# Strassen's seven products in three of eight row steps of an encoder layer's gate and up matrices, with PSUM, buffers and partial sums rearranged for it

## The chip, the cores and the metric

The kernel runs on one core of a Trainium2 chip. The metric is the time of one execution on the device in microseconds (us); the time of a kernel is the median of several runs. The profile was taken of one further execution. TensorE (PE) does the matmuls, VectorE (DVE) and ScalarE (ACT) the elementwise work, GpSimd (POOL) and SyncE (SP) issue DMAs, and POOL also does a few powers.

## The reference

The input is `x` of 256 rows and 2048 columns in float32. The layer is an FFN, a mixer with two attentions, and an FFN again, each with a norm before and after it. Cut to what matters here:

```python
def swiglu(h, w_gate, w_up, w_down):          # w_gate, w_up: 2048 x 5632, w_down: 5632 x 2048
    return (jax.nn.silu(h @ w_gate) * (h @ w_up)) @ w_down

f = swiglu(rmsnorm(x, ffn1_pre_g), ffn1_w_gate, ffn1_w_up, ffn1_w_down)
x = x + 0.5 * rmsnorm(f, ffn1_post_g)
h = rmsnorm(x, mix_pre_g)
proj = h @ w_in                               # 2048 x 8704: q, k, v of both attentions, gates ga, gb
...
merged = ga * (out_a @ w_proj_a) + gb * (out_b @ w_proj_b)
x = x + rmsnorm(merged @ w_out, mix_post_g)
f = swiglu(rmsnorm(x, ffn2_pre_g), ffn2_w_gate, ffn2_w_up, ffn2_w_down)
x = x + 0.5 * rmsnorm(f, ffn2_post_g)
```

## The kernel before

All weights come from memory once, as float32, and go through the same three steps. `load_upto` (L133) issues a DMA from SP of one unit, 256 rows by 512 columns (512 KB, as 128 partitions by 1024 elements), into one of four `raw` buffers. `emit_upto` (L142) splits the unit: ACT casts it to float32r, the high part (L152), and DVE subtracts that from the raw values, the low part (L154). Both go into the ten `w` buffers, five units. Activations are split in the same way, once, when they are transposed. A product is then three matmuls, high by high, low by high and high by low (`mm3`, L161 to L164), each of 128 x 128 activations that are loaded as weights of the array and 512 columns of the matrix that stream past.

`run_block` (L188) computes 512 columns for all 256 rows of the activations: two PSUM banks, one for each half `h` of 128 rows, and a loop over units of 256 matrix rows. A unit has two halves `j` of 128 rows, so it is 2 x 2 products, twelve matmuls. `weights(k)` emits two units ahead (`LA`). After the last unit `after(h, acc)` takes the bank: silu for a gate block (L349), the product with the silu for an up block (L353), a transposition through PSUM (`split_T`, L279 to L286), which is deferred by one unit, and so on.

`ffn` (L334) goes over the eleven column blocks of the gate and up matrices in two halves, six and five; a gate block has eight units, then the up block of the same columns. The transposed results are `hT`. After each half come four down blocks over the rows of that half. The results of the first half stay on the chip in `f` (ACT copy, L367), and those of the second are added to them on DVE (`finish_f`, L308), followed by the post norm. The mixer's 17 column blocks of `w_in`, two projections and `w_out` use `run_block` too. Its attentions are pipelines of small items that advance by one stage with each unit (`pump`).

PSUM has eight banks: four for blocks, two for transpositions, two for attention. The residual `x_sb` stays in its own buffers throughout. A scheduler orders each engine's instructions by program order as priority and by its own estimate of times; an engine then works in that order.

Of the kernel before, what the change touches and what calls it, by code (L numbers as in the profile page):

```python
# [11 lines left out]
F32 = mybir.dt.float32  # L12
# [23 lines left out]
SP0, SP1 = 3, 3  # L36
PACE0 = 5
AHEAD = 2
WARM = 7
# [3 lines left out]
def encoder_layer(  # L43
# [12 lines left out]
    xpool = ctx.enter_context(tc.tile_pool(name="xpool", bufs=1))  # L56
# [4 lines left out]
    t2p = ctx.enter_context(tc.tile_pool(name="t2p", bufs=6))  # L61
    bcp = ctx.enter_context(tc.tile_pool(name="bcp", bufs=2))
# [14 lines left out]
    def tp_tile():  # L77
        return tpp.tile([P, 4, P], F32, tag="tp", name=nm("tp"))

    def at_tile():  # L80
        return atp.tile([P, 2, 256], F32, tag="at", name=nm("at"))

    def t2():
        return t2p.tile([P, NC], F32, tag="t2", name=nm("t2"))

    def g4(shape, dt=F32R):
        return g4p.tile([P] + shape, dt, tag="g4", name=nm("g4"))
# [10 lines left out]
    x_sb = [xpool.tile([P, D], F32, name=f"x_sb{h}") for h in range(2)]  # L98
# [21 lines left out]
    def add_block(w, r0, nu, c0):  # L120
        start = len(units)
        for u in range(nu):
            units.append(w[r0 + 256 * u:r0 + 256 * u + 256, c0:c0 + NC])
        return start

# [6 lines left out]

    def load_upto(i):  # L133
        for k in range(len(loaded), min(i + 1, len(units))):
            loaded[k] = rawp.tile([P, 2, NC], F32, tag="raw", name=nm("raw"))
            c = units[k].shape[1]
            dst = loaded[k].rearrange("p a b -> p (a b)").rearrange("p (j c) -> p j c", c=c)
            src = units[k].rearrange("(j p) c -> p j c", p=P)
            for j in range(2) if k == 0 else (slice(None),):
                nc.sync.dma_start(dst[:, j], src[:, j])  # L140

    def emit_upto(i):  # L142
        for k in range(len(emitted), min(i + 1, len(units))):
            load_upto(k)
            raw = loaded[k]
            if k in spill:
                hi, lo = g4([2, NC]), g4([2, NC])
            else:
                hi = wp.tile([P, 2, NC], F32R, tag="w", name=nm("whi"))
                lo = wp.tile([P, 2, NC], F32R, tag="w", name=nm("wlo"))  # L150
            for j in range(2) if k == 0 else (slice(0, 2),):
                nc.scalar.copy(hi[:, j], raw[:, j])  # L152
                with queued(lo_of.get(0) if k in paced else None):
                    nc.vector.tensor_tensor(lo[:, j], raw[:, j], f32(hi[:, j]), ALU.subtract)  # L154
            emitted[k] = (hi, lo)
# [32 lines left out]
    def run_block(start, nu, lhs, after, lag=0, pre=None, tail=None):  # L188
        acc = [acc_tile(), acc_tile()]
        for i in range(nu + lag):  # L190
# [12 lines left out]
            for h, u in ((0, i), (1, i - lag)):  # L203
                if not 0 <= u < nu:
                    continue
                whi, wlo = weights(start + u)
                t = lhs(u, h)
                for j in range(2):
                    mm3(acc[h], t[:, 0, j, :], t[:, 1, j, :], whi[:, j, :], wlo[:, j, :],
                        u == 0 and j == 0, u == nu - 1 and j == 1)  # L210
                if u == nu - 1:
                    after(h, acc[h])
            pump()

    def quad(t, u):
        return t[:, :, 2 * (u % 2):2 * (u % 2) + 2, :]
# [14 lines left out]
    def make_xT(gi):  # L231
        done = set()

        def pre(u, h):
# [24 lines left out]
            if u % 2:  # L259
# [8 lines left out]
                else:  # L268
                    later(sq, 2)
# [9 lines left out]
    def split_T(src, n, name_shape):  # L279
# [3 lines left out]
        t = g4(name_shape)  # L283
        nc.scalar.copy(t[:, 0, :, :], tp[:, 0:n, :])  # L284
        nc.vector.tensor_tensor(t[:, 1, :, :], tp[:, 0:n, :], f32(t[:, 0, :, :]), ALU.subtract)  # L285
        return t  # L286

    def load_bc(src):
        t = bcp.tile([P, NC], F32, tag="bc", name=nm("bc"))
# [3 lines left out]
    def post_norm(f, r, h, final):  # L293
        def add_cols(c0, w):
            nc.vector.scalar_tensor_tensor(  # L295
                x_sb[h][:, c0:c0 + w], f[h][c0 // (2 * NC)][:, c0 % (2 * NC):c0 % (2 * NC) + w],
                r, x_sb[h][:, c0:c0 + w], ALU.mult, ALU.add)
# [4 lines left out]
        else:  # L302
            upd[h] = lambda u: add_cols(u * 256, 256)

    def finish_f(acc, f, gb, ss, h, n, add_prev, mul, add, final):
        fv = f[h][n // 2][:, (n % 2) * NC:(n % 2) * NC + NC]
# [27 lines left out]
    def ffn(post_g, pre, plan, lag, final, tail):  # L334
        hT = {}

        f = [[g4([2 * NC], F32) for _ in range(2)] for _ in range(2)]
        ss = [small(4, f"fss{h}") for h in range(2)]

        def lhs_h(off):  # L340
            return lambda u, h: quad(hT[(off + u) // 2, h], off + u)

        for half, (c_lo, c_hi) in enumerate(((0, 6), (6, 11))):
            for c in range(c_lo, c_hi):
                s = [None, None]

                def gate_after(h, acc, s=s):
                    s[h] = t2()
                    nc.scalar.activation(s[h], acc, AF.Silu, scale=r_pre[h])  # L349

# [405 lines left out]
```

## Time and profile before

| | |
|---|---|
| median of 3 runs | 2082.71 us (2082.37 to 2083.48) |
| the profiled execution | 2083.59 us |
| its span, first to last instruction | 2081.2 us |
| PE busy | 2064.4 us |
| DVE busy | 1141.7 us |
| ACT busy | 948.8 us |
| POOL busy | 24.5 us |
| moved by DMA | 393.40 MB |

Busy time is the time in which an engine executes instructions. A matmul's record lasts longer than the distance to the next one, because matmuls are pipelined; the rate is the distance between starts. An engine's idle time before an instruction is given with what ended it.

### The profile page before, as it was taken

Reading aid. Unit: us, or ns where it says so; the run is one execution under the profiler, and the core shown is the slowest. Engines: PE = TensorE matmul, PEld = TensorE weight load, DVE = VectorE, ACT = ScalarE, POOL = GpSimd, SP = SyncE. Lnnn points to the kernel's source line nnn. Section 1 sums busy time; section 2 is a strip of 40 time slices with the busy share of each in tenths; the row PEclk is TensorE's granted clock in tenths of the full one; section 3 lists DMA queues with packets and bytes.
Section 4 is the critical chain, followed back from the end, with each engine's and each line's share of the span. In section 5 each row is a group of like instructions: output and inputs, shape, how many; then the busy total and the mean of one; then the engine's idle time right before and its main releaser. Section 6 shows DMA issues by size and latency. Waiting matters only on the chain.

```text
span 2081.2 us, 24436 instructions
## 1 busy us (share of the span) xinstructions
PE 2064.4 (99%) x9373; PEld 1708.8 (82%) x9373; DVE 1141.7 (55%) x1330; ACT 948.8 (46%) x1205; POOL 24.5 (1%) x41
## 2 busy tenths in 40 slices
PE   9999999999999999999999999999999999999998
PEld 6888888888888878888888888888888888888886
DVE  5554444444445576767755555664445444455455
ACT  6444444444444455554644444554444444444442
POOL 1000000000000000000000000000000000000000
PEclk9999999999999999999999999999999999999999
DMA  8666655566665655555466666566665556666563
GB/s 258 200 189 186 192 192 192 192 193 190 189 189 196 198 168 187 171 163 172 152 196 198 197 204 198 182 193 191 192 191 188 189 196 193 189 189 191 187 204 125
DMA packets 203749, 393.40 MB, mean 189 GB/s; under 512 B 12447, under 2 KB 13265, under 8 KB 203633
## 3 DMA queue, kind: packets, MB, share of 16 engines
q1 hardware_dynamic: 203216, 391.17, 59.6%
q8 instruction: 73, 1.20, 0.2%
q0 software_dynamic: 384, 0.68, 0.2%
q14 instruction: 44, 0.35, 0.0%
q10 hardware_dynamic: 32, 0.01, 0.0%
HBM read 389.71 MB, written 2.10 MB: 188 GB/s over the span
## 4 chain that ended last, share of the span: by engine, by line
PE 63%; issue 34%; DMA 1%; DVE 1%; ACT 1%; POOL 0%; POOLq 0%; DVEq 0%; ACTq 0%
PE acc L163 20%; PE acc L164 20%; PE acc L162 20%; PE tp L282 1%; DMA raw<-in_w_in 0%; PE at L162 0%; PE at L163 0%; PE at L164 0%; DVE x_sb L295 0%; PE tp L246 0%; DMA sink<-in_sink_logit 0%; ACT whi L152 0%; DMA raw<-in_ffn_w_down 0%; DMA raw<-in_ffn_w_up 0%; DVE g L154 0%
## 5 line engine op out<-in xcount | busy, mean ns | idle before, releaser
L154 DVE TENSOR_TENSOR wlo<-raw,whi 128x1024 fp32r<-128x1024 f32 (+1 forms) x715 | 874.1, 1223 | 853.0 <-ACT whi L152 842.1
L152 ACT CAST whi<-raw 128x1024 fp32r<-128x1024 f32 (+1 forms) x715 | 752.0, 1052 | 974.6 <-PE acc L163 928.6
L163 PE MATMUL acc<-whi,xT 128*128 128x512 f32 x1928 | 754.1, 392 | 0.7 <-DVE xT L254 0.6
L162 PE MATMUL acc<-whi,xT 128*128 128x512 f32 x1928 | 754.1, 392 | 0.2 <-ACT whi L152 0.2
L164 PE MATMUL acc<-wlo,xT 128*128 128x512 f32 x1928 | 753.5, 392 | 0.0
L163 PEld LDWEIGHTS acc<-whi,xT 128*128 128x128 f32 x1928 | 362.7, 188 | 75.1 <-DVE xT L254 1.7
L162 PEld LDWEIGHTS acc<-whi,xT 128*128 128x128 f32 x1928 | 362.7, 188 | 74.1 <-ACT xT L252 0.8
L164 PEld LDWEIGHTS acc<-wlo,xT 128*128 128x128 f32 x1928 | 362.8, 188 | 73.1 <-DVE wlo L154 0.3
L162 PE MATMUL acc<-whi,g 128*128 128x512 f32 x928 | 361.3, 389 | 0.0
L163 PE MATMUL acc<-whi,g 128*128 128x512 f32 x928 | 361.3, 389 | 0.0
L164 PE MATMUL acc<-wlo,g 128*128 128x512 f32 x928 | 361.2, 390 | 0.0
L164 PEld LDWEIGHTS acc<-wlo,g 128*128 128x128 f32 x928 | 174.2, 188 | 36.2
L163 PEld LDWEIGHTS acc<-whi,g 128*128 128x128 f32 x928 | 174.2, 188 | 36.0
L162 PEld LDWEIGHTS acc<-whi,g 128*128 128x128 f32 x928 | 174.2, 188 | 35.9
L285 DVE TENSOR_TENSOR g<-tp,g 128x512 fp32r<-128x512 f32 (+1 forms) x68 | 42.2, 653 | 19.3 <-ACT g L284 19.3
L284 ACT CAST g<-tp 128x512 fp32r<-128x512 f32 (+1 forms) x68 | 35.4, 563 | 36.8 <-PE tp L282 36.4
L252 ACT ACTIVATE xT<-tp,gT 128x128 fp32r<-128x128 f32 x96 | 29.6, 367 | 25.7 <-PE tp L246 25.4
L349 ACT ACTIVATE t<-acc,pnr 128x512 f32<-128x512 f32 x44 | 30.2, 686 | 10.5 <-PE acc L164 10.5
L282 PE MATMUL tp<-ident,t 128*128 128x128 f32 x256 | 34.6, 272 | 0.0
L282 PEld LDWEIGHTS tp<-ident,t 128*128 128x128 f32 x256 | 30.2, 140 | 5.2
L254 DVE SCALAR_TENSOR_TENSOR xT<-tp,gT,xT 128x128 fp32r<-128x128 f32 x96 | 28.8, 344 | 8.3 <-ACT xT L252 7.5
L353 DVE SCALAR_TENSOR_TENSOR t<-acc,pnr,t 128x512 f32<-128x512 f32 x44 | 32.4, 748 | 0.0
(138 smaller groups left out, 598.7 us busy)
## 6 DMA issues: line engine op xcount, KB each, us to landing
raw<-in_ffn_w_up SPq DMA_DIRECT2D x176, 512.0 KB, 3.5
raw<-in_ffn_w_down SPq DMA_DIRECT2D x176, 512.0 KB, 3.8
raw<-in_ffn_w_gate SPq DMA_DIRECT2D x175, 512.0 KB, 3.5
raw<-in_w_in SPq DMA_DIRECT2D x136, 512.0 KB, 3.7
raw<-in_w_out SPq DMA_DIRECT2D x32, 512.0 KB, 4.5
raw<-in_w_proj_b SPq DMA_DIRECT2D x16, 512.0 KB, 4.3
raw<-in_w_proj_a SPq DMA_DIRECT2D x16, 512.0 KB, 4.4
bc<-in_ffn_post_g SPq DMA_DIRECT2D x8, 256.0 KB, 4.5
```

What stands on the lines that cost most here:

```text
L152: nc.scalar.copy(hi[:, j], raw[:, j])
L154: nc.vector.tensor_tensor(lo[:, j], raw[:, j], f32(hi[:, j]), ALU.subtract)
L162: nc.tensor.matmul(o, lhi, rhi, start=first, stop=False)
L163: nc.tensor.matmul(o, llo, rhi, start=False, stop=False)
L164: nc.tensor.matmul(o, lhi, rlo, start=False, stop=last)
L252: hi_of[h] = nc.scalar.activation(t[:, 0, j, :], tp[:, j, :], AF.Copy, scale=gs[j])
L254: lo_of[h] = nc.vector.scalar_tensor_tensor(t[:, 1, j, :], tp[:, j, :], gs[j], f32(t[:, 0, j, :]), ALU.mult, ALU.subtract)
L282: nc.tensor.transpose(tp[:, j, :], src[:, j * P:(j + 1) * P], ident)
L284: nc.scalar.copy(t[:, 0, :, :], tp[:, 0:n, :])
L285: nc.vector.tensor_tensor(t[:, 1, :, :], tp[:, 0:n, :], f32(t[:, 0, :, :]), ALU.subtract)
L349: nc.scalar.activation(s[h], acc, AF.Silu, scale=r_pre[h])
L353: nc.vector.scalar_tensor_tensor(hh, acc, r_pre[h], s[h], ALU.mult, ALU.mult)
```

## The change

The weight unit becomes 1 MB, 2048 elements a partition, in one of three kinds: `T` is 512 rows by 512 columns, `N` is 256 rows by 1024 columns, and `S` is also 256 rows by 1024 columns, but in four pieces of 128 x 512 for a Strassen step. There are four `raw` buffers and six `w` buffers, three units.

`run_wide` computes 1024 columns for all 256 rows: four results of 128 x 512. A plain step (`N`) is eight products, 24 matmuls. A Strassen step (`S`) takes the activations' and the weights' 2 x 2 pieces, and does seven products, 21 matmuls, into seven banks, with sums of the weight pieces (three additions on DVE, then the split) and sums of the activations' pieces (`make_forms`, once for each FFN and step). The products of all three Strassen steps of a block accumulate in the same banks, and the plain steps accumulate into four of them, since those are part of the four results. After the last `S` step, one copy on ACT and eight operations on DVE combine the banks in place, with priority, and the last two plain steps add onto the result.

Gate and up columns 512 to 5631 are done as five pairs of column blocks with the steps `NSNSNSNN`; column block 0 stays in `run_block`. Most other blocks become wide with plain steps alone. The down matrix is done in three parts of rows (column blocks 0 to 2, 3 to 6, 7 to 10) where there were two halves; the results of the first two parts go to memory, the second with an accumulating DMA, and are loaded before the third. `x` is loaded again from memory where it is needed, and after the post norm is written there. All PSUM tiles come from one pool of eight banks. The attention items and gates of the mixer are reordered; their computation stays. The diff, cut to its core:

```diff
+SKIND = "NSNSNSNN"
+HP = 300
+PARTS = ((0, 3), (3, 7), (7, 11))
-    wp = ctx.enter_context(tc.tile_pool(name="wp", bufs=10))
-    g4p = ctx.enter_context(tc.tile_pool(name="g4p", bufs=20))
+    wp = ctx.enter_context(tc.tile_pool(name="wp", bufs=6))
+    bigp = ctx.enter_context(tc.tile_pool(name="bigp", bufs=9))
-    accp = ctx.enter_context(tc.tile_pool(name="accp", bufs=4, space=bass.MemoryType.PSUM))
-    tpp = ctx.enter_context(tc.tile_pool(name="tpp", bufs=2, space=bass.MemoryType.PSUM))
-    atp = ctx.enter_context(tc.tile_pool(name="atp", bufs=2, space=bass.MemoryType.PSUM))
+    accp = ctx.enter_context(tc.tile_pool(name="accp", bufs=8, space=bass.MemoryType.PSUM))
...
     def emit_upto(i):
...
+            split(hi, lo, slice(0, 3))
+            nc.vector.tensor_tensor(raw[:, 1::2], raw[:, 1:3], raw[:, 3:4].to_broadcast([P, 2, NC]), ALU.add)
+            nc.vector.tensor_tensor(raw[:, 2], raw[:, 2], raw[:, 1], ALU.add)
+            nc.vector.tensor_tensor(raw[:, 0], raw[:, 0], raw[:, 2], ALU.add)
+            thi, tlo = pair("big")
+            split(thi, tlo, slice(0, 4))
+            emitted[k] = (hi, lo, thi, tlo)
...
+    def run_wide(block, lhs, forms, after):
...
+        for u, kind in enumerate(kinds):
+            w = weights(start + u)
+            if kind == "S":
+                t = lhs(u, 0), lhs(u, 1)
+                a11, a12, a22 = [(t[h][:, 0, j, :], t[h][:, 1, j, :]) for h, j in ((0, 0), (0, 1), (1, 1))]
+                fm = forms(u)
+                s1, s2, s3, s4 = [(fm[:, 0, i, :], fm[:, 1, i, :]) for i in range(4)]
+                ops = {"P1": (a11, w[0:2], 1), "P2": (a12, w[0:2], 0), "P3": (s4, w[0:2], 2),
+                       "Q5": (s1, w[2:4], 1), "P7": (s3, w[2:4], 3), "P6": (s2, w[2:4], 2), "Q4": (a22, w[2:4], 0)}
+                order = ("P1", "P2", "P6", "Q5", "P3", "P7", "Q4") if u == last_s else ("P1", "P2", "P3", "Q5", "P7", "P6", "Q4")
+                for o in order:
+                    f = open_(o)
+                    mm3s(bank[o], *ops[o], f, u == last_s, True)
+                if u == last_s:
+                    with tc.high_priority(HP):
+                        a, u2, v = t2(), t2(), t2()
+                        nc.scalar.copy(a, bank["P1"])
+                        nc.vector.tensor_tensor(bank["P2"], bank["P2"], a, ALU.add)
+                        nc.vector.tensor_tensor(u2, bank["P6"], a, ALU.add)
+                        nc.vector.tensor_tensor(v, bank["Q5"], u2, ALU.subtract)
+                        nc.vector.tensor_tensor(bank["P3"], bank["P3"], v, ALU.add)
+                        nc.vector.tensor_tensor(u2, bank["P7"], u2, ALU.add)
+                        if "X" in bank:
+                            nc.vector.tensor_tensor(v, bank["Q5"], u2, ALU.subtract)
+                            nc.vector.tensor_tensor(bank["X"], bank["X"], v, ALU.add)
...
+                        nc.vector.tensor_tensor(bank["Q4"], bank["Q4"], u2, ALU.add)
+            else:
+                order = (("P2", 0, 0), ("P3", 0, 1), ("X", 1, 1), ("Q4", 1, 0)) if last_s >= 0 else (("P2", 0, 0), ("P3", 0, 1), ("Q4", 1, 0), ("X", 1, 1))
+                for o, h, c in order:
+                    t = lhs(u, h)
+                    for j in range(2):
+                        f = open_(o)
+                        closes = u == end or u == last_s - 1 and o == "X"
+                        mm3s(bank[o], (t[:, 0, j, :], t[:, 1, j, :]), w, 2 * j + c, f, closes and j == 1, last_s >= 0)
+                    if u == end:
+                        with tc.high_priority(HP):
+                            after(h, c, bank[o])
             pump()
...
+    def reload_x(src):
+        for h in range(2):
+            x_sb[h] = big([D], F32)
+            nc.gpsimd.dma_start(x_sb[h], src[h])
...
+                later(tr, 2 if c0 + 1 in last_c or c0 == 0 else len(SKIND) - 1)
...
+            def down_after(h, c, acc, n, gb):
+                if not xlast:
+                    t = t2()
+                    nc.scalar.copy(t, acc)
+                    nc.gpsimd.dma_start(f_dram[h][:, (n + c) * NC:(n + c + 1) * NC], t,
+                                        accum_op=ALU.add if part else ALU.bypass)
+                else:
+                    finish_f(acc, f, gb[c], ss[h], h, n + c, True, 4.0 / D, 4.0 * EPS, final)
+            if xlast:
+                for h in range(2):
+                    f[h] = big([D], F32)
+                    nc.gpsimd.dma_start(f[h], f_dram[h])
```

`make_forms` does five additions or subtractions on DVE, one cast on ACT and one subtraction on DVE for each Strassen step, all of 512 elements a partition or less. The units that are split early at the border to the next stage (`spill`) were six of 512 KB and are one of 1 MB, and those held back (`paced`) were three and are one.

## Rows read from the trace of the kernel before

**Rows 1.** The page: busy time, share of the span and instructions of each engine.

```profile
PE 2064.4 (99%) x9373; PEld 1708.8 (82%) x9373; DVE 1141.7 (55%) x1330; ACT 948.8 (46%) x1205; POOL 24.5 (1%) x41
```

**Rows 2.** By stretch: us, busy PE, PEld, DVE, ACT, POOL, clock, DMA share, GB/s.

```profile
64.00:108.50 44.50, 44.50 (x202) 36.89 (x201) 22.37 (x21) 20.39 (x21) 0.00 (x0) 1.00 0.62 190
108.50:153.00 44.50, 44.50 (x202) 36.95 (x201) 22.38 (x21) 19.21 (x20) 0.00 (x0) 1.00 0.61 190
```

**Rows 3.** Order of time, PE: start us, duration us, line, tile; 36 matmuls apart.

```profile
100.09 0.39 PE L163 MATMUL acc<-whi,xT 128*128 128x512 f32 x1
...
108.25 0.39 PE L163 MATMUL acc<-whi,xT 128*128 128x512 f32 x1
```

**Rows 4.** The chain that ended last: two groups of transposes, start us, us.

```profile
64.19 0.87 PE tp L282 x8
108.64 0.87 PE tp L282 x8
```

**Rows 5.** Waits: who waited for whom, us in total, times, longest us.

```profile
ACT whi L152 <- PE acc L163: 928.6, 602, 2.6
DVE wlo L154 <- ACT whi L152: 842.1, 625, 2.5
...
PE acc L163 <- DVE xT L254: 2.2, 4, 0.8
```

**Rows 6.** By stretch, as rows 2: the start, the border to the mixer, the end.

```profile
0.00:20.00 20.00, 16.81 (x56) 10.61 (x57) 8.37 (x22) 11.02 (x26) 2.03 (x9) 1.00 0.90 304
720.00:760.00 40.00, 38.03 (x174) 30.24 (x173) 29.29 (x54) 20.31 (x37) 3.81 (x4) 1.00 0.54 172
...
2060.00:2081.00 21.00, 10.81 (x48) 8.63 (x46) 10.76 (x18) 0.00 (x0) 3.58 (x4) 0.87 0.29 100
```

**Rows 7.** Groups by shape: count, busy us, mean ns, idle before, releaser.

```profile
L154 DVE TENSOR_TENSOR wlo<-raw,whi 128x1024 fp32r<-128x1024 f32 x713 | 872.7, 1225 | 852.6 <-ACT whi L152 841.7 <-PE tp L282 5.9 <-PE at L164 0.9
...
L152 ACT CAST whi<-raw 128x1024 fp32r<-128x1024 f32 x713 | 750.7, 1054 | 972.4 <-PE acc L163 928.6 <-issue 21.8 <-ACT g L689 3.9
...
L353 DVE SCALAR_TENSOR_TENSOR t<-acc,pnr,t 128x512 f32<-128x512 f32 x44 | 32.4, 748 | 0.0
...
L308 DVE TENSOR_TENSOR g<-acc,g 128x512 f32<-128x512 f32 x16 | 11.0, 687 | 9.0 <-PE acc L164 8.7
...
L367 ACT COPY g<-acc 128x512 f32<-128x512 f32 x16 | 9.3, 583 | 4.3 <-PE acc L164 4.3
...
L481 DVE TENSOR_TENSOR t<-t,t 128x512 f32<-128x512 f32 x12 | 8.0, 683 | 0.0
...
L154 DVE TENSOR_TENSOR wlo<-raw,whi 128x512 fp32r<-128x512 f32 x2 | 1.4, 692 | 0.4 <-ACT whi L152 0.4
...
L152 ACT CAST whi<-raw 128x512 fp32r<-128x512 f32 x2 | 1.2, 619 | 2.2 <-DMA raw<-in_ffn_w_gate 2.2
```

**Rows 8.** Order of time, ACT and DVE: start us, duration, shape, idle time before.

```profile
101.19 1.05 ACT L152 CAST whi<-raw 128x1024 fp32r<-128x1024 f32 x1 [1.67 <-PE acc L163]
102.28 1.23 DVE L154 TENSOR_TENSOR wlo<-raw,whi 128x1024 fp32r<-128x1024 f32 x1 [1.50 <-ACT whi L152]
...
718.91 0.68 DVE L314 TENSOR_TENSOR g<-g,bc 128x512 f32<-128x512 f32 x1
719.52 0.15 DVE L316 TENSOR_REDUCE fss<-fss 128x1 f32<-128x3 f32 x1
...
724.97 1.23 DVE L154 TENSOR_TENSOR g<-raw,g 128x1024 fp32r<-128x1024 f32 x1 [1.69 <-ACT g L152]
726.12 1.22 DVE L154 TENSOR_TENSOR wlo<-raw,whi 128x1024 fp32r<-128x1024 f32 x1
```

**Rows 9.** DMA issues: out, in, queue, count, KB each, median us to landing.

```profile
raw<-in_ffn_w_up SPq DMA_DIRECT2D x176, 512.0 KB, 3.5
...
x_sb<-in_x SPq DMA_DIRECT2D x2, 512.0 KB, 9.2
...
rope<-in_c_rope POOLq DMA_DIRECT2D x1, 256.0 KB, 4.1
```

More of the change, by code (lines that the diff above doesn't have):

```diff
@@ L118, in encoder_layer, with add_units, add_tall, add_wide @@
     units = []
-    def add_block(w, r0, nu, c0):
+    def add_units(w, r0, rows, c0, kinds):
         start = len(units)
-        for u in range(nu):
-            units.append(w[r0 + 256 * u:r0 + 256 * u + 256, c0:c0 + NC])
-        return start
+        r = r0
+        for k in kinds:
+            n, c = (512, NC) if k == "T" else (256, 2 * NC)
+            units.append((k, w[r:r + n, c0:c0 + c]))
+            r += n
+        assert r == r0 + rows
+        return start
+    def add_tall(w, r0, rows, c0):
+        return add_units(w, r0, rows, c0, "T" * (rows // 512))
+    def add_wide(w, r0, rows, c0, kinds=None):
+        kinds = kinds or "N" * (rows // 256)
+        return add_units(w, r0, rows, c0, kinds), kinds
     loaded, emitted = {}, {}
@@ new lines, in run_block, with mm3s, open_ @@
+            if i % 2:
+                pump()
+    def mm3s(o, t, w, q, first, last, skip=False):
+        nc.tensor.matmul(o, t[0], w[0][:, q, :], start=first, stop=False, skip_group_check=skip)
+        nc.tensor.matmul(o, t[1], w[0][:, q, :], start=False, stop=False, skip_group_check=skip)
+        nc.tensor.matmul(o, t[0], w[1][:, q, :], start=False, stop=last, skip_group_check=skip)
+    def run_wide(block, lhs, forms, after):
+        start, kinds = block
+        last_s = kinds.rfind("S")
+        bank, opened = {}, set()
+        end = len(kinds) - 1
+        def open_(o):
+            if o not in bank:
+                bank[o] = acc_tile()
+            f = o not in opened
+            opened.add(o)
+            return f
+        for u, kind in enumerate(kinds):
[24 more added lines that the diff above has]
+                        else:
+                            nc.vector.tensor_tensor(bank["P1"], bank["Q5"], u2, ALU.subtract)
+                            bank["X"] = bank["P1"]
+                            opened.add("X")
+                        nc.vector.tensor_tensor(bank["Q4"], bank["Q4"], u2, ALU.add)
+            else:
+                order = (("P2", 0, 0), ("P3", 0, 1), ("X", 1, 1), ("Q4", 1, 0)) if last_s >= 0 else                     (("P2", 0, 0), ("P3", 0, 1), ("Q4", 1, 0), ("X", 1, 1))
+                for o, h, c in order:
+                    t = lhs(u, h)
+                    for j in range(2):
+                        f = open_(o)
[4 more added lines that the diff above has]
+                            after(h, c, bank[o])
@@ L453, in gains_T @@
             nc.vector.tensor_scalar_mul(gT[:, 48:50], gT[:, 48:50], 1.0 - LAM_INIT)
[L454 to L456 removed]
+        later(gains_T, 4)
+    later(constants, 4)
     pres = [make_xT(i) for i in range(3)]
     pres[0](0, 0)
[L459 removed]
+    ffn(ffn1_post_g, pres[0], plan1, 0, False, pres[1], [x_in[h * P:(h + 1) * P, :] for h in range(2)])
     roper = {}
```

441 lines of the change are left out of this document (247 added, 194 removed).

## The prediction

> **What bounds the kernel now.** I read the page's first two parts, then the table by stretch, then TensorE's own order of time, then the groups by shape, then the waits. The page gives TensorE (PE) 99% of the span, VectorE (DVE) 55% and ScalarE (ACT) 46% [rows 1]. That share is a mean, so I looked at the stretches where the change lies: there PE is busy for the whole of each, at a granted clock of 1.00, the higher of its two levels (2.4 GHz), with DVE busy half of the time [rows 2]. A busy PE could still be a slow one, so the cadence decides: the matmuls that start at 100.09 and 108.25 us are 36 apart, (108.25 - 100.09) / 36 = 0.2267 us each, without a gap [rows 3]. One gate block and one up block are 192 matmuls, 192 x 0.2267 = 43.5 us, and 0.87 for eight transposes makes 44.4; the distance of two such groups of transposes is 44.45 [rows 4]. So in these stages a matmul less is 0.2267 us less, as long as its operands come in time. The waits say that they do: ACT's casts wait for PE to give up weight buffers and DVE's subtractions for ACT, 929 and 842 us in all, while PE itself hardly appears as a waiting engine [rows 5]. PE is idle only at the start, by 2 us between the first FFN and the mixer, and at the end [rows 6].
>
> The profiled execution took 2083.59 us, 2.4 more than its span of 2081.2, and 0.9 more than the median of the runs shown. I make the sum against it.
>
> **What goes.** Gate and up columns 512 to 5631 are done in pairs of 512: five pairs, two matrices, two FFNs, 20 wide blocks. Three of their eight row steps use seven products where the plain step has eight; a product is three matmuls. That is 20 x 3 x 3 = 180 matmuls, 180 x 0.2267 = 40.8 us of PE [rows 3]. Nothing else on PE changes in number: the other wide blocks do the same matmuls in another order, and transposes and attention stay. 2083.6 - 40.8 = 2042.8.
>
> A page speaks for a smaller gain: the Trainium skill, "TensorE: Matmul & The Clock Gate", section "Wait — 56ns, not 53.3ns?", gives a warm start-to-start time of columns over 2.4 GHz plus about 2.5 ns, 215.7 ns at 512 columns, by which the 180 would be 38.8 us. The row has 226.7 ns at the same granted clock, so the trace disagrees and decides.
>
> **What DVE gets.** A row step now reads 256 x 1024 weights, 2048 elements a partition. The trace has no such shape; 512 and 1024 elements take 0.692 and 1.225 us [rows 7], so 512 more cost 0.533, and 1536 and 2048 come to 1.76 and 2.29. A plain step's low part: 2.29. A Strassen step: low parts of three of four pieces 1.76, three additions (1024, 512 and 512 elements, 1.225 + 0.683 + 0.683), low parts of the four sums 2.29: 6.65. A block has 5 x 2.29 + 3 x 6.65 = 31.4 us. At its last Strassen step eight operations combine the products, 8 x 0.687 = 5.5; their price stands on sums that read PSUM [rows 7], and writing PSUM is not in the trace, so 0.6 to 0.9 each. An up block adds four products with silu (0.748), and their four low parts after transposition (0.687, PSUM read too): 5.7. Gate and up together: 62.8 + 11.0 + 5.7 = 79.5 us of DVE. PE in that time: 2 x (5 x 24 + 3 x 21) = 366 matmuls, 83.0 us, and 1.7 of transposes: 84.7. So DVE stands at 94% by durations, where it is near 50% now.
>
> Durations overstate it. Where DVE is not kept waiting, a 512 operation that lasts 0.68 is followed 0.61 us later by the next, and a 1024 one after 1.15 [rows 8]. At these intervals the pair is some 75 us, 89%. The Trainium skill, "VectorE: DVE Perf Modes", section "The DRAIN you can't avoid", says that the next operation does not start until the pipe is empty; by that 79.5 would stand, and what could slip is 5 us a pair, not 10. The row sides with the shorter interval. Either way DVE's sum lies beside PE; ACT's does too: 1.92 a plain step, 1.49 + 1.92 a Strassen one (0.435 per 512 elements from 0.619 and 1.054 [rows 7]), 39.7 a pair, and with a dozen shorter casts and copies (0.583 to 0.619) under 50 of 84.7.
>
> **What can come late.** A sum that fits says nothing of the order. A Strassen step's chain is: ACT cast 1.49, DVE low 1.76, additions 2.4 at the intervals above, ACT cast of the sums 1.92, DVE low 2.29, and four handovers of 0.04, the time from the end of a cast to the next subtraction [rows 8]: 10.0 us. Weight buffers hold three row steps, so it starts when PE leaves the step three earlier: one plain and one Strassen step ahead, 45 x 0.2267 = 10.2 us. The sums are needed only after three products (2.0 us), or two in a block's last Strassen step (1.4), and their low part two matmuls later (0.45): slack 2.7 and 2.0 us. But DVE must fit the next plain step's 2.29 in too, and ACT its 1.92 cast; that cast starts 4.8 us in, ends at 6.7, the cast of the sums follows to 8.6, the plain low part ends at 9.0, the sums' low part at 11.3. The slack is then 0.7 us in the last Strassen step of a block and 1.4 in the others. After an up block the four silu products stand in front as well, and DVE ends its chain at about the time that the first Strassen step needs it. DVE is in order: behind each such chain stand the next low parts, and PE behind those.
>
> The combination is read by PE again: the plain step after it adds onto the combined banks. P1 and P2 are done 1.4 us into the last Strassen step and the first bank is needed at 4.8; the eight operations end about 7.9 if one plain low part got in ahead, where the fourth bank is asked for at 8.8, but the third only just in time, 7.3 against 7.5. So nothing to a microsecond a block.
>
> I take one DVE operation (0.4 us, between nothing and the 0.61 of a short one) late in each of 20 blocks, 8 us, and 2 us for the borders of blocks. The bounds: nothing, if the order fits everywhere; 60 x 0.61 = 37 us if every Strassen step comes one short operation late.
>
> **The rest, at nothing.** The forms of the activations: three steps, six DVE operations each, about 8 us an FFN, while DVE idles for half of an ordinary up block [rows 2]; without that cover 8 us. Partial sums go from ACT to memory by 32 DMAs of 256 KB from POOL's queue, where before 16 ACT copies (0.583) kept them on the chip [rows 7]. Accumulation in a DMA is in no row; plain 256 KB from the same queue took 4.1 us [rows 9]. They have a whole part, over 160 us, until the next accumulation, and the reload has a wide block, 43 us, where 512 KB of x took 9.2 at the crowded start [rows 9]. POOL's queue holds besides them only single-column powers. About 24 MB on 393 take the share of DMA time from 0.61 to 0.66 [rows 2]. A 1 MB load is between 3.5 us and twice that [rows 9]; the buffer of a Strassen step is free 1 to 2 us after PE enters it, and its successor is wanted over 8 us later. The tall first block loads 512 rows at once: the start is at 304 GB/s and bound by loads [rows 6], as many bytes come in almost the same order: 0, from -2 to +3. The border to the mixer has two large early units instead of twelve small: 0, from -1 to +4. Eight shared PSUM banks: a plain block holds four and hands over four, three of them early: 0 to 0.5 us in some 30 blocks.
>
> **Rivals.**
> (1) The gain is half eaten: DVE is late by 0.3 to 0.55 us in each of 60 steps, or the combination by 1.5 us in 20 blocks. 18 to 33 us: 2061 to 2077. For it: a slack of 0.7 us at 89 to 94% load. Against: the chain does not need DVE's whole lead in two of three steps.
> (2) Slower: DVE becomes the bound, by one mechanism. If in DVE's order a plain low part and its wait for the cast stand ahead of the sums (2.3 us), or the chain starts a short operation late each time, and the time is not won back because DVE's load leaves 0.9 us a Strassen step, each Strassen step holds PE. It saves 0.68 us, so from 0.68 us of delay a step the kernel is slower; at 1.2, 60 x 1.2 = 72: 2115. Against: DVE now idles 1.5 us before a subtraction, waiting for the cast and not for work [rows 8], and the room at the two plain steps that end a block makes good what was lost.
> (3) It gives nothing: the delays come to 0.6 to 0.75 us a step, 2079 to 2087.
>
> **How the numbers follow.** Forecast: 2083.6 - 40.8 + 10 = 2052.8, less 0.9 for the median: 2052, its own range 2041 to 2062, chance 0.56. Rival 1 has 0.25, rival 3 0.06, rival 2 0.12, and 0.01 lies below 2041. The range 2041 to 2076 takes in the forecast and nearly all of rival 1, about 0.8. A measurement of this kernel can tell 0.2%, 4.2 us, from no change: faster 0.82, same 0.06, slower 0.12.
>
> **What would show it.** PE's count down by 180 and its cadence in a gate block still 0.2267; about 85 us from pair to pair of gate and up where it is 88.9; DVE's busy time up from 1142 to about 1470 us, ACT's to about 1000; combining operations near 0.69 us. Delays of steps appear as PE waiting for DVE's sums at the first product that uses them, and as fewer casts waiting for PE; the combination appears as PE waiting for a DVE write of a bank. I am wrong if the interval of matmuls grows, if the operations into PSUM cost much over 0.9 us, if PE waits for DMA in the wide blocks, or if the gaps stand in stages that I set at nothing.

## The result and the profile after

| | before | after |
|---|---|---|
| median | 2082.61 us (2082.37 to 2083.48) | 2101.51 us (2097.97 to 2102.28) |
| after over before | | 1.0087, interval 1.0069 to 1.0104 |
| profiled execution | 2083.59 us | 2102.28 us |
| its span | 2081.2 us | 2100.5 us |

The forecast was 2052 with a range to 2076. The kernel became slower by 19 us, so forecast and range are both wrong.

The page after, as [rows 1] and [rows 9]: busy time of each engine, the DMA totals, and two groups of DMA issues (count, KB each, median us to landing).

```profile
PE 2045.2 (97%) x9193; PEld 1680.1 (80%) x9193; DVE 1430.9 (68%) x1400; ACT 987.4 (47%) x943; POOL 56.2 (3%) x91
...
DMA packets 140571, 416.36 MB, mean 198 GB/s; under 512 B 8415, under 2 KB 9233, under 8 KB 139185
...
raw<-in_ffn_w_down SPq DMA_DIRECT2D x88, 1024.0 KB, 5.2
...
f_dram<-t POOLq DMA_DIRECT2D x32, 256.0 KB, 5.8
```

PE has 9193 matmuls, 180 fewer. DVE rose to 1431 us and ACT to 987; 1470 and 1000 were forecast. 23 MB more were moved, where 24 were forecast. So the kernel does what the change says. The groups by shape of after, as [rows 7] (count, busy us, mean ns of one, idle time before and what ended it):

```profile
L179 DVE TENSOR_TENSOR w<-raw,w 128x2048 fp32r<-128x2048 f32 x301 | 689.1, 2289 | 416.5 <-ACT w L177 409.9 <-PE acc L258 5.1
L177 ACT CAST w<-raw 128x2048 fp32r<-128x2048 f32 x301 | 575.8, 1913 | 665.7 <-PE acc L258 513.8 <-PE acc L201 71.9 <-issue 37.8
...
L179 DVE TENSOR_TENSOR w<-raw,w 128x1536 fp32r<-128x1536 f32 x60 | 105.3, 1755 | 83.7 <-ACT w L177 55.9 <-issue 27.8
...
L188 DVE TENSOR_TENSOR raw<-raw 128x1024 f32<-128x1024 f32 x60 | 73.3, 1221 | 0.8
...
L190 DVE TENSOR_TENSOR raw<-raw 128x512 f32<-128x512 f32 x60 | 41.3, 688 | 0.9
...
L293 DVE TENSOR_TENSOR acc<-acc,t 128x512 f32<-128x512 f32 x20 | 13.9, 693 | 0.0
```

The prices that were worked out from smaller shapes hold: 2.29, 1.76, 1.22 and 0.69 us. An operation that writes PSUM in place takes 0.693, as one that only reads it did. The cadence holds too. In PE's order of time, these two matmuls of wide gate and up blocks are 332 apart, plain and Strassen steps between them (start us, duration):

```profile
249.86 0.39 PE L258 MATMUL acc<-w,xT 128*128 128x512 f32 x1
...
325.12 0.39 PE L259 MATMUL acc<-w,big 128*128 128x512 f32 x1
```

(325.12 - 249.86) / 332 = 0.2267 us, as [rows 3]. Not one price was wrong. What was wrong is the time that PE loses, idle or at the lower clock. The table by stretch of after, as [rows 2, 6] (us, busy PE, PEld, DVE, ACT, POOL, granted clock, DMA share, GB/s):

```profile
75.00:100.00 25.00, 21.37 (x86) 16.61 (x85) 20.29 (x15) 15.73 (x12) 0.00 (x0) 0.93 0.69 233
350.00:375.00 25.00, 25.00 (x112) 20.71 (x111) 24.69 (x18) 17.71 (x12) 0.00 (x0) 1.00 0.47 156
625.00:650.00 25.00, 23.06 (x95) 18.60 (x94) 21.18 (x19) 9.83 (x6) 2.17 (x4) 0.93 0.86 325
725.00:750.00 25.00, 21.23 (x87) 16.64 (x87) 17.48 (x26) 8.80 (x8) 4.03 (x4) 0.91 0.61 211
1000.00:1025.00 25.00, 18.52 (x84) 14.66 (x83) 16.72 (x21) 8.81 (x6) 0.00 (x0) 0.94 0.57 191
1425.00:1450.00 25.00, 21.33 (x80) 16.32 (x80) 19.46 (x17) 11.44 (x8) 0.00 (x0) 0.86 0.73 252
2079.00:2100.00 21.00, 8.64 (x39) 6.82 (x37) 10.00 (x18) 0.00 (x0) 3.57 (x4) 0.77 0.29 100
```

In 350 to 375 DVE is busy for 24.69 of 25 us, and PE is still never idle. The larger losses of this table are in single places: the first wide pair of each FFN (75, 1425), the first down weights after a wide block (625), the border to the mixer (725), one place in the mixer (1000), and the end.

To put a number on each stage I summed, over PE's whole order of time, the distance from start to start less 0.2267 us for each matmul of 512 columns, half of that for one of 256, and 0.109 for each transposition (0.87 / 8 [rows 4]). This is PE's lost time, whether it idles or runs at the lower clock. The stages are the start (to 50 us), the two FFNs, the border to the mixer, the mixer, and the border to the second FFN; a border lasts from 5 us before the first transposition of the rows for the next norm to 1 us after the last. The end is from the last matmul's start. All in us, profiled executions; the kernels e1 to e11 come below.

| | before | after | e1 | e2 | e3 | e4 | e5 | e6 | e11 |
|---|---|---|---|---|---|---|---|---|---|
| start | 9.3 | 9.9 | 9.5 | 9.8 | 10.3 | 10.8 | 9.9 | 9.8 | 9.4 |
| FFNs | 0.7 | 35.9 | 0.5 | 23.5 | 20.2 | 34.4 | 16.3 | 0.5 | 51.1 |
| border to mixer | 3.7 | 10.2 | 10.7 | 7.6 | 11.7 | 9.6 | 7.3 | 7.9 | 7.3 |
| mixer | 2.5 | 13.3 | 13.3 | 12.6 | 13.3 | 9.2 | 2.7 | 2.7 | 2.7 |
| border to FFN 2 | 2.0 | 6.5 | 6.8 | 6.7 | 6.5 | 6.6 | 6.3 | 6.7 | 6.4 |
| sum | 18.1 | 75.8 | 40.7 | 60.1 | 62.1 | 70.5 | 42.6 | 27.6 | 76.9 |
| end | 10.8 | 13.3 | 13.2 | 12.9 | 13.5 | 13.2 | 12.8 | 12.8 | 12.2 |

From before to after: 57.6 more lost (75.77 - 18.14), 2.5 more at the end, 40.8 saved: +19.3, the difference of the spans.

### The profile page after: what moved, and what is told of

It is laid out like the page before. It is cut to its first block, busy times and chain, and to the rows that moved or that the text cites. A ratio compares the mean times of both kernels' runs of the same rounds, so it can differ in the third digit from the quotient of the medians.

```text
span 2100.5 us, 22846 instructions
## 1 busy us (share of the span) xinstructions
PE 2045.2 (97%) x9193; PEld 1680.1 (80%) x9193; DVE 1430.9 (68%) x1400; ACT 987.4 (47%) x943; POOL 56.2 (3%) x91
## 5 line engine op out<-in xcount | busy, mean ns | idle before, releaser
L179 DVE TENSOR_TENSOR w<-raw,w 128x2048 fp32r<-128x2048 f32 (+2 forms) x365 | 796.5, 2184 | 500.3 <-ACT w L177 465.8
L177 ACT CAST w<-raw 128x2048 fp32r<-128x2048 f32 (+2 forms) x365 | 666.7, 1828 | 783.8 <-PE acc L258 605.4
L257 PE MATMUL acc<-w,xT 128*128 128x512 f32 x1368 | 536.6, 393 | 5.6 <-ACT t L292 4.0
L258 PE MATMUL acc<-w,xT 128*128 128x512 f32 x1368 | 534.1, 390 | 0.0
L259 PE MATMUL acc<-w,xT 128*128 128x512 f32 x1368 | 512.5, 391 | 0.6 <-DVE w L179 0.6
L257 PE MATMUL acc<-w,big 128*128 128x512 f32 x828 | 323.2, 391 | 3.3 <-ACT w L177 3.3
L258 PE MATMUL acc<-w,big 128*128 128x512 f32 x828 | 323.8, 391 | 0.0
L259 PE MATMUL acc<-w,big 128*128 128x512 f32 x828 | 317.6, 390 | 0.2 <-DVE w L179 0.2
L257 PEld LDWEIGHTS acc<-w,xT 128*128 128x128 f32 x1368 | 257.5, 188 | 61.9 <-ACT t L292 4.8
L259 PEld LDWEIGHTS acc<-w,xT 128*128 128x128 f32 x1368 | 257.5, 188 | 54.8 <-DVE w L179 1.4
L258 PEld LDWEIGHTS acc<-w,xT 128*128 128x128 f32 x1368 | 257.6, 188 | 52.0
L257 PEld LDWEIGHTS acc<-w,big 128*128 128x128 f32 x828 | 155.7, 188 | 36.4 <-ACT w L177 4.1
L259 PEld LDWEIGHTS acc<-w,big 128*128 128x128 f32 x828 | 155.6, 188 | 32.5 <-DVE w L179 0.6
L258 PEld LDWEIGHTS acc<-w,big 128*128 128x128 f32 x828 | 155.7, 188 | 31.9
L177 ACT CAST big<-raw 128x2048 fp32r<-128x2048 f32 x62 | 118.6, 1913 | 93.1 <-DVE raw L190 89.1
L179 DVE TENSOR_TENSOR big<-raw,big 128x2048 fp32r<-128x2048 f32 x62 | 141.2, 2286 | 20.7 <-ACT big L177 15.8
L201 PE MATMUL acc<-w,xT 128*128 128x512 f32 x208 | 83.0, 401 | 3.0 <-DVE xT L358 3.0
L200 PE MATMUL acc<-w,xT 128*128 128x512 f32 x208 | 82.0, 399 | 0.0
L202 PE MATMUL acc<-w,xT 128*128 128x512 f32 x208 | 80.4, 393 | 0.0
L257 PE MATMUL acc<-big,big 128*128 128x512 f32 x180 | 72.3, 402 | 6.1 <-ACT big L177 6.1
L200 PE MATMUL acc<-w,big 128*128 128x512 f32 x192 | 74.7, 389 | 0.0
L201 PE MATMUL acc<-w,big 128*128 128x512 f32 x192 | 74.7, 389 | 0.0
```

What stands on the lines that cost most here:

```text
L177: nc.scalar.copy(hi[:, sl], raw[:, sl])
L179: nc.vector.tensor_tensor(lo[:, sl], raw[:, sl], f32(hi[:, sl]), ALU.subtract)
L200: nc.tensor.matmul(o, lhi, rhi, start=first, stop=False)
L201: nc.tensor.matmul(o, llo, rhi, start=False, stop=False)
L202: nc.tensor.matmul(o, lhi, rlo, start=False, stop=last)
L257: nc.tensor.matmul(o, t[0], w[0][:, q, :], start=first, stop=False, skip_group_check=skip)
```

## The experiments

Each is an edit of the changed kernel and does the whole computation. Each is measured against the kernel before on the same chip in the same session (medians of before: 2082.50 for e1 to e4, 2082.41 for e5 to e8, 2082.09 for e9 to e11).

### e1: the rearrangement alone

```diff
-SKIND = "NSNSNSNN"
+SKIND = "NNNNNNNN"
```

> All eight row steps of every gate and up pair are plain (the step string is NNNNNNNN), all else as in the changed kernel. Theory A: PE's time in the gate and up pairs falls by 40.8 us of matmuls and rises by some 27 us of stalls there, and the rearrangement outside the Strassen steps costs some 32 us; so without Strassen 2101.5 + 40.8 - 27 = 2115 (2111 to 2119). Rival B: the whole loss comes from the load that Strassen puts on DVE, and the rearrangement is free: 2083 (2079 to 2088).

Measured: 2109.07 us (2107.98 to 2109.16), 1.0124 of before, 1.0109 to 1.0139. So everything but Strassen's products costs 26.6 us, and Strassen's 180 matmuls less bring 2109.07 - 2101.51 = 7.6 us instead of 40.8. The table by stretch of e1:

```profile
75.00:100.00 25.00, 25.00 (x112) 20.70 (x111) 9.84 (x5) 9.02 (x5) 0.00 (x0) 1.00 0.56 182
625.00:650.00 25.00, 25.00 (x112) 20.70 (x111) 10.91 (x5) 7.96 (x5) 0.00 (x0) 1.00 0.52 181
1000.00:1025.00 25.00, 20.43 (x93) 16.34 (x91) 15.92 (x19) 8.81 (x6) 0.00 (x0) 0.98 0.57 191
```

The FFNs are full again (0.5 in the table of stages, 0.7 before), also at 625, where the partial sums are loaded back. The mixer's hole stays, and so do the borders and the end. Two causes, then: 35 us of lost PE time (75.8 - 40.7) that comes with Strassen's steps, and 25 that comes with the rest (40.7 - 18.1, and 2.4 at the end). Rival B, a free rearrangement, is out; theory A had it right in kind, with 2111 at the least.

### e3: the forms of the activations earlier

```diff
-                    gate_up(0, ..., lambda a: run_block(plan["up"][0], KU, lhs_x, a))
-                    make_forms(SKIND)
+                    def first_up(a):
+                        make_forms(SKIND)
+                        run_block(plan["up"][0], KU, lhs_x, a)
+                    gate_up(0, ..., first_up)
```

> The sums of the activations' pieces (make_forms) are written ahead of the first up block instead of behind it, all else as in the changed kernel. Theory A: the stalls in the first wide pair of each FFN, some 6 us each with the lower clock that follows, come from these 8 us of DVE work falling together with the first Strassen steps: 2089 to 2093. Rival B: the first pair is slow by its own chain or its loads, not by the forms: 2099 to 2102.

Measured: 2088.50 us (2087.17 to 2090.94), 1.0027 of before, 1.0018 to 1.0037: 13.0 us less than after. DVE's order of time shows when the last low part of the forms ends, first in after, then in e3:

```profile
79.03 0.68 DVE L402 TENSOR_TENSOR big<-t,big 128x512 fp32r<-128x512 f32 x1
```

```profile
55.04 0.69 DVE L402 TENSOR_TENSOR big<-t,big 128x512 fp32r<-128x512 f32 x1
```

The prediction hid these 8 us in the half-idle DVE of the first up block. But the change writes them behind that block, and program order is the scheduler's priority: in after, the first of them starts at 60.80 and they run between the sums of the first wide block. That block then gets its own operations late. DVE, then ACT, then PE of after (in brackets, the idle time before and what ended it):

```profile
88.87 2.29 DVE L179 TENSOR_TENSOR w<-raw,w 128x2048 fp32r<-128x2048 f32 x1
91.08 0.69 DVE L190 TENSOR_TENSOR raw<-raw 128x512 f32<-128x512 f32 x1
91.68 2.29 DVE L179 TENSOR_TENSOR w<-raw,w 128x2048 fp32r<-128x2048 f32 x1
```

```profile
89.44 1.90 ACT L177 CAST w<-raw 128x2048 fp32r<-128x2048 f32 x1 [0.75 <-DMA raw<-in_ffn_w_up]
91.24 0.58 ACT L292 COPY t<-acc 128x512 f32<-128x512 f32 x1
91.80 1.90 ACT L177 CAST big<-raw 128x2048 fp32r<-128x2048 f32 x1
```

```profile
91.87 0.50 PE L257 MATMUL acc<-w,xT 128*128 128x512 f32 x1 [2.19 <-ACT t L292]
...
93.75 0.79 PE L257 MATMUL acc<-big,big 128*128 128x512 f32 x1 [1.14 <-ACT big L177]
```

A whole low part (2.29) stands ahead of the last sum, L190, and the sums' cast follows that. A whole cast (1.90) stands ahead of the copy that PE waits for. In e3 PE loses 0.7 us in 75 to 100 and nothing in 1425 to 1450; in after it lost 5.9 and 6.8 there.

### e4: no empty pipeline ahead of the attention items

```diff
     run_wide(pm["qa"], lhs_x, None, q_after(qaT))
-    drain()
     ticker[0] = pipeline([ItemA(h, p) for h in range(2) for p in range(4)], (0, 1, 2))
```

> The drain after the qa block is left out, so that the transposes of its four results come one step of the next block later; all else as in the changed kernel. Theory A: the 9.4 us that PE loses there wait for four rotations on DVE that nothing covers; with a step of 5.4 us ahead of them, 5 to 8 us come back: 2093 to 2097. Rival B: the rotations only move and PE waits as long behind the step: 2100 to 2102.

Measured: 2095.98 us (2094.69 to 2096.93), 1.0060 of before, 1.0044 to 1.0077: 5.5 us less than after. `drain` does all deferred work before the items start: the transpositions of four rotated results, with no matmuls of a block between them. PE and DVE of after at that place:

```profile
1018.01 0.66 PE L407 MATMUL tp<-ident,t 128*128 128x128 f32 x4 [1.10 <-DVE t L648]
1021.46 0.82 PE L407 MATMUL tp<-ident,t 128*128 128x128 f32 x4 [2.80 <-DVE t L648]
1024.86 1.97 PE L407 MATMUL tp<-ident,t 128*128 128x128 f32 x8 [2.58 <-DVE t L648]
```

```profile
1020.72 0.68 DVE L648 TENSOR_TENSOR t<-t,t 128x512 f32<-128x512 f32 x1
1021.32 2.29 DVE L179 TENSOR_TENSOR w<-raw,w 128x2048 fp32r<-128x2048 f32 x1
```

Three waits on DVE, 6.5 us, and in the last of them a whole low part stands ahead of the next rotations. The line is not new: in the kernel before, the same `drain` stands behind the second of two blocks of 512 columns, and its transpositions (974.28 and 975.49) wait for nothing. The change put one wide block with four rotations ahead of it. Without `drain` PE is busy for all of 1000 to 1025. The mixer's stage gives 4.1 of the 5.5 us; 1.5 stand in the FFNs, which the edit doesn't touch. Some of the gain is given back in the attention items, where a small operation now has a whole low part ahead of it (e4, DVE, then PE):

```profile
1075.39 2.28 DVE L179 TENSOR_TENSOR w<-raw,w 128x2048 fp32r<-128x2048 f32 x1
...
1077.66 0.42 DVE L807 TENSOR_TENSOR big<-at,big 128x256 fp32r<-128x256 f32 x1
```

```profile
1078.23 0.51 PE L200 MATMUL at<-t,big 128*128 128x256 f32 x1 [2.70 <-DVE big L807]
```

### e2, e7, e9: smaller pieces of the split

e2 casts and subtracts 1024 elements at a time, as before the change, while loads and steps stay as they are. e7 halves the subtractions alone, e9 the casts alone. The core of e2:

```diff
-                for j in ... if k == 0 else [slice(0, 4)]:
+                for j in ... if k == 0 else [slice(0, 2), slice(2, 4)]:
                     split(hi, lo, j)
...
-            split(hi, lo, slice(0, 3))
+            split(hi, lo, slice(0, 2))
+            split(hi, lo, slice(2, 3))
...
-            split(thi, tlo, slice(0, 4))
+            split(thi, tlo, slice(0, 2))
+            split(thi, tlo, slice(2, 4))
```

and of e7 (e9 does the same to the cast in place of the subtraction):

```diff
                 nc.scalar.copy(hi[:, sl], raw[:, sl])
-                with queued(lo_of.get(0) if k in paced else None):
-                    nc.vector.tensor_tensor(lo[:, sl], raw[:, sl], f32(hi[:, sl]), ALU.subtract)
+                for a in range(sl.start, sl.stop, 2):
+                    q = slice(a, min(a + 2, sl.stop))
+                    with queued(lo_of.get(0) if k in paced else None):
+                        nc.vector.tensor_tensor(lo[:, q], raw[:, q], f32(hi[:, q]), ALU.subtract)
```

> Casts and subtractions of the weights in pieces of 1024 elements, as in the kernel before, instead of 2048; loads, steps and all else as in the changed kernel. Theory A: a part of the stalls comes from pieces of 2.29 us that stand in DVE's order ahead of a short operation that PE waits for; halving them gives back a third to a half of the 56 us of stalls added: 2075 to 2090. Rival B: DVE's load decides; more operations make it higher: 2101 to 2106.

> DVE's subtractions of the weights in pieces of 1024 elements, ACT's casts left at 2048; all else as in the changed kernel. Theory A: it is DVE's long piece ahead of short operations that costs: most of e2_halves' 15 us comes back, 2087 to 2092. Rival B: it is the length of the chain, in which a subtraction waits for a whole cast: casts of 2048 leave it as it was, 2096 to 2102.

> ACT's casts of the weights in pieces of 1024 elements, DVE's subtractions left at 2048, the counterpart of e7_dve_halves; all else as in the changed kernel. Theory A: what helps is that a subtraction of the first half runs beside the cast of the second, which shortens the chain and needs both halved: 2099 to 2103. Rival B: it is ACT's long cast that stands ahead of short casts and copies: most of e2_halves' 15 us comes back, 2086 to 2092.

Measured: e2 2086.37 us (2084.84 to 2087.88), 1.0017 of before, 1.0008 to 1.0027, 15.1 less than after, though DVE's busy time rose by 27 us to 1458. e7 2102.37 (2101.68 to 2104.17), 1.0096, 1.0080 to 1.0111; e9 2100.35 (2099.03 to 2102.82), 1.0085, 1.0070 to 1.0100: no gain from either alone. After e2 I held that DVE's long pieces ahead of short operations are the whole cause. By that e7 should have had most of e2's gain, so that theory fell.

The stages tell more than the medians. The FFNs lose 28.9 us in e7 and 27.7 in e9, against 35.9 in after and 23.5 in e2. Each half alone does help there, by 7 to 8 us, and the mixer takes most of it back: 20.2 in e7 and 19.5 in e9, against 13.3. DVE, then PE of e7 at the largest of these places:

```profile
965.80 2.72 DVE L838 SCALAR_TENSOR_TENSOR t<-acc,pnr,t 128x512 f32<-128x512 f32 x4
968.43 2.35 DVE L181 TENSOR_TENSOR w<-raw,w 128x1024 fp32r<-128x1024 f32 x2
...
971.57 0.48 DVE L738 TENSOR_SCALAR t<-at,br 128x256 f32<-128x256 f32 x1 [0.47 <-POOL br L329]
```

```profile
972.11 0.69 PE L748 MATMUL tp<-ident,t 128*128 128x128 f32 x2 [4.67 <-DVE t L738]
```

Two halves in a row are no shorter than a whole when nothing is put between them (2.35 us here, 2.29 for a whole). The edit changed the scheduler's order, and at this place to a worse one: four gate operations and both halves ahead of the 0.48 us for which PE waits (4.67; in after 1.48). What can be said is that pieces of 1024 on both engines bring 15 us, of which the FFNs have 12 and the borders and the mixer 3. With both halved, the subtraction of the first half can run beside the cast of the second. How much of e2's gain is that shorter chain and how much is a luckier order, these three runs don't separate.

### e5 and e6: the three together, and with plain steps

e5 has the edits of e2, e3 and e4; e6 has them and the SKIND of e1.

> The three edits together: pieces of 1024 elements, forms ahead of the first up block, no drain after the qa block. Theory A: they cure different stalls, so the gains add: 2101.5 - 15.1 - 13.0 - 5.5 = 2068 (2064 to 2073), below the kernel before. Rival B: the first two cure the same stalls (late chains in the first wide pairs), so that about half of the smaller is lost: 2074 to 2081.

> As e5_three, with plain steps alone. Theory A: in good order the Strassen steps lose little of their 40.8 us of matmuls, some 10 us; plain steps are then about 30 us slower than e5_three: 2095 to 2100. Rival B: DVE's load in the Strassen blocks eats the gain whatever the order, as it did at 2109 against 2101.5: 6 to 14 us slower than e5_three.

Measured: e5 2069.59 us (2068.65 to 2070.30), 0.9937 of before, 0.9924 to 0.9949; e6 2093.93 (2093.18 to 2094.79), 1.0054, 1.0040 to 1.0068. The three gains add up in the total, 15.1 + 13.0 + 5.5 = 33.6 against 31.9 measured, and the change becomes a gain: 12.8 us, where the forecast had 31. That the total came out is luck in part, since theory A's reason doesn't hold by stage. In the FFNs the three gain 12.4, 15.7 and 1.5 us apart, 29.6, and 19.6 together: there they cure the same stalls, as rival B had it. In the mixer they gain 4.8 apart and 10.6 together. Strassen's steps now bring 2093.93 - 2069.59 = 24.3 us of 40.8; the FFNs still lose 16.3. The first row of PE's waits in e5 (us in total, times, longest):

```profile
PE acc L261 <- DVE big L179: 5.1, 9, 0.6
```

Nine short waits for the sums' low part, of 0.5 to 0.6 us: this is the late operation that the prediction priced. e6 still stands 11.5 us above before. By the table of stages that is the borders (4.2 and 4.7) and the end (2.0), and the mixer has no part in it any more (0.2).

### e8 and e10: the end and the borders

e8 splits the last unit early; e10 is e8 and lets the second half of the rows lag by three steps where it was two.

```diff
         spill.add(b)
         paced.add(b + 3)
+    spill.add(len(units) - 1)
```

```diff
-LAG = 2
+LAG = 3
```

> As e5_three, and the last weight unit of the kernel is split into buffers of its own, as the last ones of the kernel before were. Theory A: the first half of the rows is finished earlier ahead of the second, and the tail of 13.2 us from the last matmul to the end comes back to the 10.8 of before: 2 to 3 us less than e5_three. Rival B: the tail is set by DVE's order there and not by the unit: as e5_three, within 1 us.

> As e8_three_spill, with a lag of three row steps instead of two between the halves of the rows at the two borders into the next norm. Theory A: PE waits at the borders because too few matmuls of the second half lie behind the first half's norm (10 to 14 where before there were 18); six more matmuls give 1 to 1.4 us at each border: 2066 to 2068. Rival B: the weights of three units leave no buffer for the next, so that the gain is lost again or more: 2069 to 2074.

Measured: e8 2069.12 us (2067.66 to 2069.58), 0.9933 of before, 0.9920 to 0.9945; it can't be told from e5. Its end takes 12.0 us where that of e5 takes 12.8, less than theory A's 2 to 3. e10 2070.97 (2070.51 to 2072.44), 0.9948, 0.9936 to 0.9961; no gain. In e10 the border to the mixer lost 6.9 us (8.7 in e8), the one to the second FFN 10.1 (6.7). So neither the last unit's split nor the lag mends what is left there. The rows show what PE waits for at the border; DVE, then PE of after:

```profile
739.22 2.29 DVE L179 TENSOR_TENSOR w<-raw,w 128x2048 fp32r<-128x2048 f32 x1 [0.84 <-ACT w L177]
741.43 0.68 DVE L443 TENSOR_TENSOR big<-acc,big 128x512 f32<-128x512 f32 x1
```

```profile
746.18 1.11 PE L350 MATMUL tp<-ident,big 128*128 128x128 f32 x4 [3.73 <-DVE big L421]
```

The last addition to `f`, L443, stands behind a whole low part, and norm, residual and transposition follow it. In e2 and e5, with half pieces, the same wait is still 2.6 us. Before the change 18 matmuls of the second half of the rows stood behind the last of the first; after, 10. That this is why the rest stays is argued, not shown.

### e11: a fourth Strassen step

e8 with one step more, 60 matmuls less, 13.6 us.

```diff
-SKIND = "NSNSNSNN"
+SKIND = "SNSNSNSN"
```

> As e8_three_spill, with four Strassen steps of eight (SNSNSNSN) instead of three: 60 matmuls less, 13.6 us, and DVE's work in a gate and up pair up from 75 us to 84 by intervals, for 81.7 of PE. Theory A: at three steps the order was what cost, and at four DVE is the bound: the 13.6 us are lost to some 3 us a pair and to the shorter time for the combination: 2069 to 2090. Rival B: DVE's load never was near the bound, and the gain goes on: 2056 to 2062.

Measured: 2088.81 us (2087.86 to 2090.07), 1.0032 of before, 1.0020 to 1.0044: 19.7 slower than e8. The FFNs lose 51.1 us where e8 lost 16.1. The table by stretch, then DVE, PE and PE's longest wait in total, at the last Strassen step of a gate block:

```profile
300.00:325.00 25.00, 25.00 (x112) 20.66 (x112) 25.00 (x30) 13.98 (x16) 0.00 (x0) 1.00 0.52 173
```

```profile
340.49 0.68 DVE L190 TENSOR_TENSOR raw<-raw 128x512 f32<-128x512 f32 x1
341.09 1.22 DVE L179 TENSOR_TENSOR w<-raw,w 128x1024 fp32r<-128x1024 f32 x1
342.23 0.69 DVE L296 TENSOR_TENSOR t<-acc,t 128x512 f32<-128x512 f32 x1
```

```profile
342.97 2.82 PE L409 MATMUL tp<-ident,t 128*128 128x128 f32 x12 [2.74 <-DVE t L296]
```

```profile
PE tp L409 <- DVE t L296: 11.0, 4, 2.7
```

DVE has no idle time left in 300 to 325, yet PE loses nothing there. At 340.49 to 342.23 a sum and a low part stand ahead of a combining operation, and PE waits for that one, four times for 2.74 us and ten times for 0.6. L296 reads the bank of one product and writes a buffer that no transposition reads; by the kernel's code all that a transposition can need from it is that bank, one of the eight that all share. So the longest waits are for a bank, behind a DVE whose order is full, and a single plain step now follows the last Strassen step and covers the combination. That DVE's load alone makes the loss, as the prediction's rival has it, is not shown: no run has the fourth step with a bank to spare or with those transpositions later.

## Why the prediction was wrong

**What goes: right.** 180 matmuls are gone and the cadence is 0.2267 us. The Trainium skill's 215.7 ns ("TensorE: Matmul & The Clock Gate", section "Wait — 56ns, not 53.3ns?") does not hold in this kernel after the change either.

**What DVE gets: right.** Shapes, combination and totals came out within 3%. At three steps of eight DVE can be busy for 24.69 of 25 us without a loss on PE. DVE's short intervals hold as well: L190 starts at 91.08 and lasts 0.69, and the next operation starts 0.60 later. The prediction took from the Trainium skill, "VectorE: DVE Perf Modes", section "The DRAIN you can't avoid", the rule that an operation does not start until the pipe is empty. It left out what ends the same paragraph, "A next op that is not held starts earlier"; the rows are as that sentence has it, and which operations are held no run here tests.

**What can come late: the term was mis-sized, 10 us forecast, 35.2 measured (35.9 - 0.7).** e3 and e2 name two errors, which overlap: 15.7 and 12.4 us of the FFNs' loss go with one edit each, 19.6 with all three. The first is the place of the forms, below. The second is that the chain was laid out for one Strassen step with every operation in the best order and only its own delay behind it. With pieces of 2.29 and 1.92 us, what stands wrongly in an engine's order delays by a whole piece, as at 88.87 to 93.75, not by the 0.4 of one short operation; that this and not the longer chain is what e2 cures is argued. A third is that only waits were priced. In e5 PE's waits in the FFNs come to 8.6 us (5.1 for the sums' low parts), near the 8 + 2 of the working, but the loss is 16.3: the other half is matmuls that start further apart behind a wait. In after the waits come to 18.8 of 35.9.

**The rest, at nothing: the step that failed most, and the one that made the kernel slower.** e1, which has no forms, measures it at 26.6 us; the forms come on top, inside the FFNs' 35.2.
- *The forms* had a cover that the order did not use. The prediction named the cover and its price without it, 8 us; e3 measured 13.0, as the first wide blocks came late with them.
- *The mixer* was not costed beyond its shared banks. Its stall of 10.8 us (13.3 - 2.5) is not mainly one of banks: in its largest place PE waits 6.5 us for rotations on DVE, and e4 takes 4.1 us off the mixer by removing a `drain`. The prediction had not followed what that line empties behind a wide block. With e2's and e3's edits beside that one it is gone (2.7 in e5).
- *The borders* were 0, from -1 to +4; they cost 6.5 and 4.5. The prediction counted units split early, not what stands ahead of the last addition on DVE; as e2 keeps 2.6 of that wait with half pieces and e10 did not mend it, the cause stays open. The end, +2.5, was not in the sum at all.
- *The start*, 0, from -2 to +3: right, +0.6. *Partial sums by DMA*: no wait of PE in after ends on the accumulation. The reload's cover holds in e1; in after ACT waits 5.45 us for a load of down weights, and PE 1.94 us for ACT at 642.50 (DMA share 0.86 in that stretch). e5 has a share of 0.97 there, and its longest wait of that kind is 2.8 us. In 625 to 650 PE loses 3.8 us in after, 0.9 in e2 and e5 and 1.5 in e3, so the load's lateness alone doesn't make the loss; that the reload delays the load is argued.

**The rivals.** Slower was given 0.12, by DVE as the bound in each Strassen step. The sign came true, the mechanism did not: with Strassen's steps the changed kernel is 7.6 us faster than without. The mechanism's order (a plain low part ahead of the sums) is seen in the first wide pair of each FFN, and a DVE without idle time only in e11, where no run separates it from the banks. The wide blocks taken alone lost 35.2 us, above the first rival's 18 to 33. That several covers fail together was no rival at all: the upper ends of the terms set at nothing, 8 for the forms, 3 and 4 for the start and the border, 15 for the banks, come to 30 us, and the range was not widened by them.

## What to carry to other kernels

An operation that is hidden "in idle time" needs two checks: that the idle time exists, and that the engine's order puts the operation there; a line moved ahead of a block was worth 13 us here. Larger pieces saved 27 us of DVE's busy time here and cost 15 us of the kernel's, as short operations that PE waits for can stand behind a whole piece and a chain of casts and subtractions gets longer. So try loads and steps that are large with elementwise work split finer than them, on both engines at once, and measure the rearrangement without the new algorithm before judging the algorithm: here that told 26.6 us of side effects from 40.8 of gain, and three small edits then made 2101.5 into 2069.6 us, 0.6% below the kernel before.

## What the runs showed of the hardware

After a stall PE pays a second time. The table by stretch of after: the hole in the mixer and what follows, then what follows a single wait of 1.94 us that ends at 642.50:

```profile
1016.00:1025.00 9.00, 2.52 (x14) 1.39 (x13) 9.00 (x16) 3.07 (x3) 0.00 (x0) 0.82 0.55 180
1025.00:1028.00 3.00, 3.00 (x12) 2.71 (x13) 2.22 (x4) 1.17 (x2) 0.00 (x0) 0.50 0.92 333
```

```profile
642.50:646.00 3.50, 3.50 (x9) 2.78 (x10) 3.50 (x4) 0.00 (x0) 0.00 (x0) 0.56 1.02 424
```

PE was busy for 2.52 of 9 us, and in the next 3 us the granted clock is 0.50, the lower level of 1.2 GHz; matmuls that start at 1027.06, 1027.48 and 1027.91 are 0.43 apart instead of 0.2267. After the wait of 1.94 us the clock is 0.56 for 3.5 us, with PE busy throughout. In the five stretches with holes that stand before the end in the table by stretch the clock is 0.86 to 0.94. A stall's price here is its length and some matmuls at half speed behind it, which the prediction's bounds left out.

The DMAs of 256 KB that write the partial sums, half of them accumulating, land after 5.8 us in the median, the one plain one of [rows 9], which reads memory, after 4.1. Loads of 1 MB land after 5.0 to 5.2 us, within the bounds of 3.5 and twice that.
